# A two-block transformer on one core: transfer scratch of 1 KB instead of 16, and the room given to more places for weights

## The chip, the core and the metric

The kernel runs on one core of one Trainium2 chip. The metric is the device time of one launch in microseconds (us), as a median of several runs. The engines are TensorE (PE, matrix products), VectorE (DVE), ScalarE (ACT), GpSimd (POOL) and SyncE (SP, which does nothing but issue transfers). Each engine works through its own queue of instructions in order; ACT and POOL can issue transfers too.

## The reference, cut to what matters

The input is a sequence of 256 tokens of width 2048. A first block with adaptive modulation, four kinds of attention and 16 experts is followed by a second block with a long convolution ("hyena"), a spatial gate and a feed-forward part. All of it is in fp32.

```python
def first_block(x, c, ...):
    c_act = jax.nn.silu(c)
    mod = c_act @ ada_w[l] + ada_b[l]                 # 2048 x 12288: the modulation
    sh1, sc1, g1, sh2, sc2, g2 = jnp.split(mod, 6, axis=-1)
    h = rmsnorm(x, norm1_g[l]) * (1.0 + sc1[:, None]) + sh1[:, None]
    x = x + g1[:, None] * token_mixer(h, w_in[l], ...)     # dilated, banded, MoBA and NSA attention
    h = rmsnorm(x, norm2_g[l]) * (1.0 + sc2[:, None]) + sh2[:, None]
    x = x + g2[:, None] * moe_ffn(h, router_w, ...)        # 16 experts, 2048 -> 512 -> 2048
    return rmsnorm(x, final_g)

def compress(t, pe, w1, w2):                          # in the NSA attention: blocks of 32 keys, step 16
    blk = (t[:, :, cidx] + pe).reshape(b, hk, n_cmp, NSA_CMP_BLOCK * hd)
    return jax.nn.gelu(blk @ w1) @ w2

def _hyena_mixer(p, conv_w, conv_b, k_f, bias):       # in the second block
    v, x1, x2 = ...
    z = x1 * _long_conv(v, k_f[:, 0], bias[0])        # rfft, times k_f, irfft
    return x2 * _long_conv(z, k_f[:, 1], bias[1])
```

## The kernel before, in words

The work of one launch runs through these stages; the times are those of the profiled execution. `phase0` (0 to about 165 us) computes the first modulation vectors and the filters of the hyena part and projects the first queries, keys and values. `mixers` (to about 630 us) does the four attentions and the output projection, and the rest of the modulation beside them. Then come the router, `overflow` (a branch that runs only where a group of experts has more tokens than fit) and `experts` (about 650 to 1265 us). `block2` does the hyena part (about 1290 to 1525 us), the gate, the merge and the feed-forward part.

A weight comes in pieces of 128 x 1024 fp32 numbers, 512 KB, and each is loaded by one transfer that SP issues in `rload` (L180) into the ring `wraw` with `nraw` = 5 places. Products in fp32 are made of three products of the parts of a number: `split` lets ACT write the upper part `whi` (L146) and DVE the rest `wlo` (L149), each with three places, and `mm3` (L158 to L160) multiplies them. A place of `wraw` is free when DVE has written `wlo`.

The modulation has its own pieces of the same size, 192 of them, in `ada_steps`: the load at L446 into one of four places of the tag `a`, then four matmuls on PE into `ps_ada` (L452), or, in some steps, DVE instead (L456). These steps are called between the steps of other work through a hook, so the loads of pieces and those of weights alternate on SP.

Before the router, `first_chunks` loads 18 weight pieces of the experts in advance: 5 into the ring and 13 into places of other tiles that are idle then. The experts' other loads follow through the ring of five.

`cmp_blocks` (L883 and on) copies keys and values so that blocks of 32 can be read, with two memsets and eight transfers on POOL into the tile `kk`. `long_conv` (L1484 and on) runs four times; it loads one set of filters `kft` by three transfers on ACT's queue (L1487: 1 MB, L1489: 254 KB, L1490: 2 KB) and multiplies it with the transformed input, by way of `cu` and `cv`, one place each.

The order on each engine is set by a scheduler that runs when the program is built: it goes by priorities and by when a place comes free in its own account. More places thus change the order also where the code reads the same. At launch the order is fixed, and only waits on other engines decide when an instruction starts. Each transfer of SP and ACT also has one of eight completion counters (`DMAHW0` to `DMAHW7` in the order with its waits), given out in turn: a transfer that gets a counter waits until the one that had it has landed.

Of the kernel before, what the change touches and what calls it, by code (L numbers as in the profile page):

```python
# [9 lines left out]
F32 = mybir.dt.float32  # L10
# [8 lines left out]
P = 128  # L19
# [120 lines left out]
class Body:  # L140
# [30 lines left out]
    def rload(self, src, kt, n, tag=None):  # L171

        if tag:
            raw = self.piece([P, 1024], tag)
        elif isinstance(self.rawring, tuple):
            pool, tag, bufs = self.rawring
            raw = pool.tile([P, 1024], F32, name="wraw", tag=tag, bufs=bufs)
        else:
            raw = self.rawring
        self.nc.sync.dma_start(raw[:, :n].rearrange("p (k n) -> p k n", k=kt), src)  # L180
        return raw
# [145 lines left out]
    def run(self):  # L327
        ctx, tc, nc, i = self.ctx, self.tc, self.nc, self.i
        self.nraw, self.nsplit = 5, 3
        self.ahead, self.turn = {}, None  # L330
        self.const = ctx.enter_context(tc.tile_pool(name="const", bufs=1, reuse_waits="tile"))
        self.res = ctx.enter_context(tc.tile_pool(name="res", bufs=1, reuse_waits="tile"))
        self.wp = ctx.enter_context(tc.tile_pool(name="wts", bufs=1, reuse_waits="tile"))
        self.rawring = (self.wp, "wraw", self.nraw)
        self.tmp = ctx.enter_context(tc.tile_pool(name="tmp", bufs=2))
        self.dram = ctx.enter_context(tc.tile_pool(name="scratch", bufs=1, reuse_waits="tile", space=DRAM))

        warm = self.tmp.tile([P, 8], F32, name="warm", tag="tms", bufs=2)
        nc.vector.memset(warm, 0.0)
        nc.scalar.activation(warm, warm, AF.Silu)  # L340
        n = 4 * P + sum(WIDTHS.values())
        vec = self.const.tile([P, n], F32, name="vec")
        nc.sync.dma_start(vec, i["p_vec"])
        self.ident, self.lt, self.iota, self.ones = (vec[:, n * P:(n + 1) * P] for n in range(4))
        self.v, n = {}, 4 * P
        for k, m in WIDTHS.items():
            self.v[k] = vec[:, n:n + m]
            n += m
        self.xT = self.res.tile([P, KD, S], F32, name="xT")

        cr = ctx.enter_context(ExitStack())
        self.rt = cr.enter_context(tc.tile_pool(name="route", bufs=1, reuse_waits="tile"))
        self.shift(self.rt)

        self.lp = cr.enter_context(tc.tile_pool(name="pieces", bufs=1, reuse_waits="tile"))
        with ExitStack() as c1:
            self.pp = c1.enter_context(tc.tile_pool(name="ps1", bufs=1, reuse_waits="tile", space=PSUM))
            self.banks = {"mm": 3, "ada": 1, "b": 4}
            self.awp = c1.enter_context(tc.tile_pool(name="awts", bufs=1, reuse_waits="tile"))
            self.phase0()  # L360
            self.mixers()
        with ExitStack() as c2:
            self.pp = c2.enter_context(tc.tile_pool(name="ps2", bufs=1, reuse_waits="tile", space=PSUM))
            self.banks = {"y": 4, "g": 1, "u": 1, "b": 2}
            self.moe()
        cr.close()
        with ExitStack() as c3:
            self.pp = c3.enter_context(tc.tile_pool(name="ps3", bufs=1, reuse_waits="tile", space=PSUM))
            self.banks = {"mm": 4, "b": 4}
            self.block2()  # L370
# [64 lines left out]
    def ada_steps(self, seg, b, dve=False):  # L435


        nc, w = self.nc, self.i["ada_w"][0]
        c0 = seg * D + b * 512
        sb = self.awp.tile([P, 512], F32, name="arow", tag="arow", bufs=1)  # L440
        ps = None if dve else self.bank("ada")
        for q in range(4):
            for h in range(2):
                k0 = 4 * q + 2 * h
                raw = self.piece([P, 2, 512], "a")
                self.last_ada = nc.sync.dma_start(raw, w[k0 * P:(k0 + 2) * P, c0:c0 + 512]  # L446
                                                  .rearrange("(k p) n -> p k n", p=P))
                for j in range(2):
                    k, r = k0 + j, raw[:, j]
                    if not dve:  # L450
                        m = 32 * (2 * h + j)
                        nc.tensor.matmul(ps[m:m + 32], self.cact[:, k], r, start=q == 0, stop=q == 3)  # L452
                    elif k == 0:
                        nc.vector.tensor_scalar(sb, r, self.cs[:, k:k + 1], None, OP.mult)
                    else:
                        nc.vector.scalar_tensor_tensor(sb, r, self.cs[:, k:k + 1], sb, OP.mult, OP.add)  # L456
            if q < 3:
                yield
        n = seg * 16 + b * 4
        bias, mod = self.v["ada_b"][:, n:n + 4], self.mod[:, seg, b * 4:b * 4 + 4]  # L460
        pt = self.bank("ada")
        if dve:
            for a in range(4):
                nc.tensor.matmul(pt[:, a:a + 1], sb[:, a * P:(a + 1) * P], self.ones[:, 0:1], start=True, stop=True)
            nc.vector.tensor_tensor(mod, pt[:, :4], bias, OP.add)
        else:
            nc.vector.tensor_copy(sb, ps)
            pt = pt.rearrange("p (a q) -> p a q", a=4)
            for a in range(4):
                nc.tensor.transpose(pt[:, a], sb[:, a * P:(a + 1) * P], self.ident)  # L470
            s = self.tmp.tile([P, 4], F32, name="adas", tag="modg", bufs=2)
            nc.vector.tensor_reduce(s, pt.rearrange("p a (j r) -> p a r j", r=32)[:, :, 0], AX.X, OP.add)
            nc.vector.tensor_tensor(mod, s, bias, OP.add)
        yield
# [408 lines left out]
    def cmp_blocks(self, n, src):  # L883

        nc, mp = self.nc, self.mp
        kk = mp.tile([P, 2, S], F32, name="kk", tag="s", bufs=3)
        nc.gpsimd.memset(kk[64:, :, 255:], 0.0)
        for h in range(2):
            nc.gpsimd.dma_start(kk[:64, h], src[h * 64:h * 64 + 64])
            nc.gpsimd.dma_start(kk[64:, h, :255], src[h * 64:h * 64 + 64, 1:])  # L890
        blk = mp.tile([P, 16, 2, 16], F32, name="blk", tag="s", bufs=3)
        nc.gpsimd.memset(blk[:, :, :, 15:], 0.0)
        for h in range(2):
            v = kk[:, h].rearrange("p (n j s) -> p s j n", s=2, j=8)[:, 0]
            for a in range(2):
                js = slice(a * 8, a * 8 + 8)
                nc.vector.tensor_tensor(blk[:, js, h, :15], v[:, :, a:a + 15],
                                        self.pe[n][:, js, None].to_broadcast([P, 8, 15]), OP.add)
        return blk
# [297 lines left out]
    def moe(self):  # L1197
        nc, tc, i = self.nc, self.tc, self.i
        with ExitStack() as c0:
            self.mp = c0.enter_context(tc.tile_pool(name="moe", bufs=1, reuse_waits="tile"))  # L1200
            mp = self.mp
            wg, wu, wd = (i["exp_w_" + n][0] for n in ("gate", "up", "down"))
            self.overflow(wg, wu, wd)

            def prepare(p, tag):

# [79 lines left out]
                return work  # L1286
            self.turn = 0
            self.experts([group(g) for g in range(4)], lambda n: (wg[n], wu[n], wd[n]), step, finish)
            self.turn = None
            sums = last["sums"]  # L1290
            self.v1, self.v2 = (self.tmp.tile([P, 8], F32, name="tms", tag="tms", bufs=2) for _ in range(2))
            row = mp.tile([2, S], F32, name="sums")
# [190 lines left out]

    def long_conv(self, o, hf, z, gate):  # L1484
        nc, hp = self.nc, self.hp
        kf = hp.tile([P, 5, 512], F32, name="kft", tag="kft", bufs=1)
        nc.scalar.dma_start(kf[:, :4], self.kf[o, hf])  # L1487

        nc.scalar.dma_start(kf[1:, 4], self.kf[o, hf, 1:, 0])  # L1489
# [11 lines left out]
        for j in range(2):  # L1501
            zr, zi = self.bank("b"), self.bank("b")
            for ps, f in ((zr, j), (zi, 2 + j)):
                for t in range(2):
                    self.mm3(ps, [x[:, t, f * P:(f + 1) * P] for x in self.F], [x[:, t] for x in zt], t == 0, t == 1)
            A, B, Dm = kf[:, j], kf[:, 2 + j], kf[:, 4 if j == 0 else 1]
            for ps, q, c1, c2, op in ((zr, zi, A, B, OP.subtract), (zi, zr, Dm, B, OP.add)):
                u = hp.tile([P, 512], F32, name="cu", tag="cu", bufs=1)
                v = hp.tile([P, 512], F32, name="cv", tag="cv", bufs=1)
                tt(u, ps, c1, OP.mult)  # L1510
                tt(v, q, c2, OP.mult)
                tt(u, u, v, op)
                f = j if op == OP.subtract else 2 + j
                self.split(yf[0][:, f], yf[1][:, f], u)
# [90 lines left out]
```

## Time and profile before

| what | us |
|---|---|
| median of 3 runs (2706.68 to 2711.35) | 2710.29 |
| the profiled execution, its own time | 2719.55 |
| its span in the trace | 2717.8 |
| PE busy in the span | 2608.4 (96%) |
| DVE busy | 1795.3 (66%) |
| ACT busy | 1334.9 (49%) |
| moved by DMA: 640.81 MB, a mean of 236 GB/s | |

A busy PE is not PE at its peak: matmuls are pipelined, and one that is counted as 0.40 us can be followed by the next after 0.23 us. Where a stage waits is therefore read from when the instructions start and from what each engine waited for, not from the busy share. The page gives the span in 40 slices of 68 us, the share of each engine in tenths, and the chain of waits that ended last. A window view gives the same for a stretch, with the mean clock that PE was granted (1.00 is full speed).

### The profile page before, as it was taken

Reading aid. Unit: us, or ns where it says so; the run is one execution under the profiler, and the core shown is the slowest. Engines: PE = TensorE matmul, PEld = TensorE weight load, DVE = VectorE, ACT = ScalarE, POOL = GpSimd, SP = SyncE. Lnnn points to the kernel's source line nnn. Section 1 sums busy time; section 2 is a strip of 40 time slices with the busy share of each in tenths; the row PEclk is TensorE's granted clock in tenths of the full one; section 3 lists DMA queues with packets and bytes.
Section 4 is the critical chain, followed back from the end, with each engine's and each line's share of the span. In section 5 each row is a group of like instructions: output and inputs, shape, how many; then the busy total and the mean of one; then the engine's idle time right before and its main releaser. Section 6 shows DMA issues by size and latency. Waiting matters only on the chain.

```text
span 2717.8 us, 43662 instructions
## 1 busy us (share of the span) xinstructions
PE 2608.4 (96%) x17355; PEld 2261.0 (83%) x17355; DVE 1795.3 (66%) x2509; ACT 1334.9 (49%) x1774; POOL 5.5 (0%) x20
## 2 busy tenths in 40 slices
PE   5998999998999999999999899999999999999997
PEld 1466888887778777776998799999999999998886
DVE  4546877877889888887777655555655555555444
ACT  2333444546777766766443444444444444443443
POOL 0000000000000000000000000000000000000000
PEclk7998999998999999999999899999999999999999
DMA  8888898983899999997554355555555656566664
GB/s 296 286 294 286 281 317 309 331 295 119 297 319 312 324 315 330 331 330 270 184 169 149 127 187 187 187 186 186 186 186 187 189 184 193 186 191 197 193 194 140
DMA packets 320083, 640.81 MB, mean 236 GB/s; under 512 B 21564, under 2 KB 35420, under 8 KB 319104
## 3 DMA queue, kind: packets, MB, share of 16 engines
q1 hardware_dynamic: 310768, 618.83, 68.5%
q10 hardware_dynamic: 8848, 18.61, 2.0%
q8 instruction: 137, 2.24, 0.3%
q0 software_dynamic: 256, 0.52, 0.1%
q14 instruction: 74, 0.61, 0.1%
HBM read 631.01 MB, written 6.35 MB: 235 GB/s over the span
## 4 chain that ended last, share of the span: by engine, by line
PE 56%; DMA 9%; DVE 6%; ACT 3%; issue 1%; ACTq 1%; DVEq 0%; SPq 0%
PE ps_mm L158 16%; PE ps_mm L160 16%; PE ps_mm L159 16%; DVE wlo L149 4%; DMA wraw<-in_exp_w_down_dram 4%; DMA wraw<-in_exp_w_up_dram 4%; ACT whi L146 3%; DMA wraw<-in_exp_w_gate_dram 2%; PE ps_u L159 1%; PE ps_u L160 1%; PE ps_u L158 1%; ACTq L1490 1%; PE ps_g L158 1%; PE ps_g L159 1%; PE ps_g L160 1%
## 5 line engine op out<-in xcount | busy, mean ns | idle before, releaser
L149 DVE TENSOR_TENSOR wlo<-wraw,whi 128x1024 fp32r<-128x1024 f32 (+1 forms) x972 | 1165.7, 1205 | 703.2 <-ACT whi L146 689.4
L146 ACT ACTIVATE whi<-wraw 128x1024 fp32r<-128x1024 f32 (+1 forms) x972 | 1012.3, 1044 | 1021.0 <-PE ps_mm L159 531.9
L158 PE MATMUL ps_mm<-hH,whi 128*128 128x256 f32 x3216 | 910.9, 283 | 9.2 <-ACT whi L146 7.8
L160 PE MATMUL ps_mm<-hH,wlo 128*128 128x256 f32 x3216 | 907.8, 283 | 4.0 <-DVE wlo L149 4.0
L159 PE MATMUL ps_mm<-hL,whi 128*128 128x256 f32 x3216 | 904.2, 281 | 0.0
L158 PEld LDWEIGHTS ps_mm<-hH,whi 128*128 128x128 f32 x3216 | 607.9, 189 | 33.3 <-ACT whi L146 15.2
L160 PEld LDWEIGHTS ps_mm<-hH,wlo 128*128 128x128 f32 x3216 | 605.5, 189 | 19.0 <-DVE wlo L149 9.3
L159 PEld LDWEIGHTS ps_mm<-hL,whi 128*128 128x128 f32 x3216 | 605.7, 188 | 5.2 <-issue 4.8
L159 PE MATMUL ps_mm<-wlo,actH 128*128 128x512 f32 x352 | 137.2, 390 | 0.0
L160 PE MATMUL ps_mm<-whi,actL 128*128 128x512 f32 x352 | 137.0, 389 | 0.0
L158 PE MATMUL ps_mm<-whi,actH 128*128 128x512 f32 x352 | 137.0, 390 | 0.0
L159 PE MATMUL ps_y<-wlo,piece 128*128 128x512 f32 x256 | 105.6, 412 | 8.5 <-DVE wlo L149 7.9
L452 PE MATMUL ps_ada<-piece,cact 128*32 128x512 f32 x512 | 102.2, 650 | 9.4 <-DMA piece<-in_ada_w_dram 8.8
L160 PE MATMUL ps_y<-whi,piece 128*128 128x512 f32 x256 | 101.3, 397 | 0.2 <-DVE piece L149 0.2
L158 PE MATMUL ps_y<-whi,piece 128*128 128x512 f32 x256 | 91.6, 398 | 2.9 <-ACT piece L146 1.9
L456 DVE SCALAR_TENSOR_TENSOR arow<-piece,cs,arow 128x512 f32<-128x512 f32 x120 | 89.4, 745 | 2.1 <-DMA piece<-in_ada_w_dram 1.3
L159 PEld LDWEIGHTS ps_mm<-wlo,actH 128*128 128x128 f32 x352 | 66.1, 188 | 14.0 <-DVE wlo L149 0.3
L158 PEld LDWEIGHTS ps_mm<-whi,actH 128*128 128x128 f32 x352 | 66.1, 188 | 13.7
L160 PEld LDWEIGHTS ps_mm<-whi,actL 128*128 128x128 f32 x352 | 66.1, 188 | 13.5
L159 PEld LDWEIGHTS ps_y<-wlo,piece 128*128 128x128 f32 x256 | 48.3, 189 | 33.4 <-DVE wlo L149 23.3
L158 PE MATMUL ps_mm<-mgH,whi 128*128 128x256 f32 x256 | 71.9, 281 | 0.0
L159 PE MATMUL ps_mm<-mgL,whi 128*128 128x256 f32 x256 | 71.9, 281 | 0.0
(447 smaller groups left out, 3497.9 us busy)
## 6 DMA issues: line engine op xcount, KB each, us to landing
wraw<-in_w_in_dram SPq DMA_DIRECT2D x224, 512.0 KB, 4.6
piece<-in_ada_w_dram SPq DMA_DIRECT2D x192, 512.0 KB, 5.0
wraw<-in_w_ffn_in_dram SPq DMA_DIRECT2D x176, 512.0 KB, 4.5
wraw<-in_exp_w_down_dram SPq DMA_DIRECT2D x125, 512.0 KB, 5.7
wraw<-in_exp_w_up_dram SPq DMA_DIRECT2D x124, 512.0 KB, 5.2
wraw<-in_exp_w_gate_dram SPq DMA_DIRECT2D x122, 512.0 KB, 5.1
wraw<-in_w_ffn_out_dram SPq DMA_DIRECT2D x88, 512.0 KB, 4.2
wraw<-in_w_out_dram SPq DMA_DIRECT2D x64, 512.0 KB, 5.1
```

What stands on the lines that cost most here:

```text
L146: self.nc.scalar.activation(dst, src, AF.Copy)
L149: self.nc.vector.tensor_tensor(dst, src, h.bitcast(F32), OP.subtract)
L158: mm(ps, a[0], b[0], start=start, stop=False)
L159: mm(ps, a[0], b[1], start=False, stop=False)
L160: mm(ps, a[1], b[0], start=False, stop=stop)
L452: nc.tensor.matmul(ps[m:m + 32], self.cact[:, k], r, start=q == 0, stop=q == 3)
L456: nc.vector.scalar_tensor_tensor(sb, r, self.cs[:, k:k + 1], sb, OP.mult, OP.add)
L1490: nc.scalar.dma_start(kf[0:1, 4], self.nyq[o, hf])
```

## The change

The program is built with 1 KB of scratch for transfers that POOL prepares in software, where it was 16 KB in each partition by default. The copies of `cmp_blocks`, the only such transfers, are issued by ACT instead, and their memsets done by DVE. The room that comes free holds: three more places for modulation pieces (tag `a2`, so seven in turn), three more places for the experts' weights (tag `wraw2`, taken in turn with the five from the end of `overflow` on), and second places for `kft`, `cu` and `cv` in the hyena part.

```diff
@@ rload
         elif isinstance(self.rawring, tuple):
             pool, tag, bufs = self.rawring
+            if self.more:
+
+                here, at = self.more
+                self.more = here, (at + 1) % (bufs + 3)
+                if at < 3:
+                    pool, tag, bufs = here, "wraw2", 3
             raw = pool.tile([P, 1024], F32, name="wraw", tag=tag, bufs=bufs)
@@ ada_steps
-                raw = self.piece([P, 2, 512], "a")
+                self.nada += 1
+                raw = (self.piece([P, 2, 512], "a") if self.nada % 7 < 4 else
+                       self.awp.tile([P, 2, 512], F32, name="piece", tag="a2", bufs=3))
@@ cmp_blocks
-        nc.gpsimd.memset(kk[64:, :, 255:], 0.0)
+        nc.vector.memset(kk[64:, :, 255:], 0.0)
         for h in range(2):
-            nc.gpsimd.dma_start(kk[:64, h], src[h * 64:h * 64 + 64])
-            nc.gpsimd.dma_start(kk[64:, h, :255], src[h * 64:h * 64 + 64, 1:])
+            nc.scalar.dma_start(kk[:64, h], src[h * 64:h * 64 + 64])
+            nc.scalar.dma_start(kk[64:, h, :255], src[h * 64:h * 64 + 64, 1:])
         blk = mp.tile([P, 16, 2, 16], F32, name="blk", tag="s", bufs=3)
-        nc.gpsimd.memset(blk[:, :, :, 15:], 0.0)
+        nc.vector.memset(blk[:, :, :, 15:], 0.0)
@@ moe
             self.overflow(wg, wu, wd)
+            self.more = mp, 0
...
-            self.turn = None
+            self.turn = self.more = None
@@ long_conv
-        kf = hp.tile([P, 5, 512], F32, name="kft", tag="kft", bufs=1)
+        kf = hp.tile([P, 5, 512], F32, name="kft", tag="kft", bufs=2)
...
-                u = hp.tile([P, 512], F32, name="cu", tag="cu", bufs=1)
-                v = hp.tile([P, 512], F32, name="cv", tag="cv", bufs=1)
+                u = hp.tile([P, 512], F32, name="cu", tag="cu", bufs=2)
+                v = hp.tile([P, 512], F32, name="cv", tag="cv", bufs=2)
@@ the build
-    nc = bacc.Bacc("TRN2", target_bir_lowering=False, num_devices=1)
+    nc = bacc.Bacc("TRN2", target_bir_lowering=False, num_devices=1, dynamic_dma_scratch_size=1024)
```

The order of the instructions also changes. First, SP's queue behind the weights of the compression (`in_nsa_cmp_w_v`), in the compressed attention; `in_ada_w` are modulation pieces, `in_w_in` the projection's weights. Before:

```order
L908 DMA wraw<-in_nsa_cmp_w_k_dram 128x8x128
L908 DMA wraw<-in_nsa_cmp_w_v_dram 128x8x128 x2
L446 DMA piece<-in_ada_w_dram 128x2x512 x2
L180 DMA wraw<-in_w_in_dram 128x2x512
L446 DMA piece<-in_ada_w_dram 128x2x512 x6
L180 DMA wraw<-in_w_in_dram 128x2x512
L446 DMA piece<-in_ada_w_dram 128x2x512 x2
L180 DMA wraw<-in_w_in_dram 128x2x512
L446 DMA piece<-in_ada_w_dram 128x2x512 x2
L180 DMA wraw<-in_w_in_dram 128x2x512 x2
L446 DMA piece<-in_ada_w_dram 128x2x512 x7
```

And now:

```order
L186 DMA wraw<-in_w_in_dram 128x16x24
L916 DMA wraw<-in_nsa_cmp_w_k_dram 128x8x128 x2
L916 DMA wraw<-in_nsa_cmp_w_v_dram 128x8x128 x2
L454 DMA piece<-in_ada_w_dram 128x2x512 x16
L186 DMA wraw<-in_w_in_dram 128x2x512
L454 DMA piece<-in_ada_w_dram 128x2x512 x2
L186 DMA wraw<-in_w_in_dram 128x2x512 x2
```

Sixteen pieces stand in one row, where five loads of w_in stood between the first sixteen.

Second, ACT's queue in the hyena part with its waits (the names in brackets; `kft` is a filter set, `kf_d` and `nyq_d` its places in memory), from the head of `block2`. Before, the first set stands alone there and the second comes behind the products of the first convolution:

```order
L1487 DMA kft<-kf_d 128x2048 [waits DVE_49]
L146 ACTIVATE yfH<-cu 128x512 [waits DVE_49]
L1489 DMA kft<-kf_d 127x512
L1490 DMA kft<-nyq_d 1x512
L146 ACTIVATE whi<-wraw 128x1024 [waits DMAHW7_49,PE_49,Activation_49]
```

And now, the second set at the head of `block2`:

```order
L1496 DMA kft<-kf_d 128x2048
L146 ACTIVATE whi<-wraw 128x1024 [waits DMAHW1_49,PE_49]
L1498 DMA kft<-kf_d 127x512 [waits DMAHW2_49]
L1499 DMA kft<-nyq_d 1x512 [waits DMAHW3_49]
L146 ACTIVATE whi<-wraw 128x1024 [waits PE_49,Activation_49]
```

The second set moved ahead of the first convolution, with loads of w_in to split behind it, and the third and the fourth stand where the second and the third stood.

Third, SP's queue ahead of the branch of `overflow`, whose first row is the load of `ovi`. Before:

```order
L180 DMA piece<-in_exp_w_down_dram 128x1024
L180 DMA piece<-in_exp_w_up_dram 128x2x512
L180 DMA wraw<-in_exp_w_gate_dram 128x2x512 x5
L1303 TENSOR_LOAD ovi
L1304 COMPARE_AND_BRANCH
```

And now:

```order
L186 DMA piece<-in_exp_w_up_dram 128x2x512
L186 DMA wraw<-in_exp_w_gate_dram 128x2x512 x5
L186 DMA wraw<-in_exp_w_up_dram 128x2x512
L1312 TENSOR_LOAD ovi
L1313 COMPARE_AND_BRANCH
```

One load of `exp_w_up` moved ahead of the branch. Fourth, ACT's queue now has the eight copies of `cmp_blocks`, each with a wait:

```order
L897 DMA kk<-piece 64x256 [waits DMAHW5_49,Activation_49]
L898 DMA kk<-piece 64x255 [waits DMAHW6_49]
L897 DMA kk<-piece 64x256 [waits DMAHW7_49]
L898 DMA kk<-piece 64x255 [waits DMAHW1_49]
L897 DMA kk<-piece 64x256 [waits DMAHW2_49,Activation_49]
L898 DMA kk<-piece 64x255 [waits DMAHW3_49]
L897 DMA kk<-piece 64x256 [waits DMAHW5_49]
L898 DMA kk<-piece 64x255 [waits DMAHW6_49]
```

They stood on POOL; the last two wait for the counters of the first two.

## Rows read from the trace of the kernel before

**Rows 1.** The page: engines' busy time, PE in tenths per slice, GB/s per slice.
```profile
PE 2608.4 (96%) x17355; PEld 2261.0 (83%) x17355; DVE 1795.3 (66%) x2509; ACT 1334.9 (49%) x1774; POOL 5.5 (0%) x20
...
PE   5998999998999999999999899999999999999997
...
GB/s 296 286 294 286 281 317 309 331 295 119 297 319 312 324 315 330 331 330 270 184 169 149 127 187 187 187 186 186 186 186 187 189 184 193 186 191 197 193 194 140
```

**Rows 2.** The page: the chain that ended last, shares of the span.
```profile
PE 56%; DMA 9%; DVE 6%; ACT 3%; issue 1%; ACTq 1%; DVEq 0%; SPq 0%
```

**Rows 3.** Waits of SP's queue, whole span: us in total, times, longest.
```profile
SPq L180 <- DVE wlo L149: 1542.1, 786, 14.9
SPq L446 <- PE ps_ada L452: 184.7, 71, 7.3
```

**Rows 4.** Windows: stretch, busy per engine (instructions), PE's clock, DMA share, GB/s.
```profile
0.00:170.00 170.00, 137.59 (x664) 61.01 (x664) 86.34 (x182) 46.36 (x77) 1.00 (x10) 0.90 0.84 293
...
200.00:250.00 50.00, 43.27 (x357) 33.92 (x355) 28.16 (x54) 15.04 (x27) 0.00 (x0) 0.86 0.90 292
...
605.00:610.00 5.00, 5.00 (x44) 4.82 (x43) 3.35 (x7) 2.32 (x5) 0.00 (x0) 1.00 1.02 383
...
640.00:660.00 20.00, 10.63 (x65) 10.41 (x66) 12.87 (x54) 7.95 (x15) 0.00 (x0) 0.63 0.09 30
...
690.00:1265.00 575.00, 553.66 (x2427) 426.26 (x2426) 486.13 (x471) 408.30 (x422) 0.00 (x0) 1.00 0.93 322
...
1020.00:1040.00 20.00, 19.54 (x84) 14.70 (x83) 17.30 (x16) 14.39 (x14) 0.00 (x0) 1.00 0.99 350
```

**Rows 5.** Groups of DVE's instructions, 690 to 1265 us, the largest.
```profile
L149 DVE TENSOR_TENSOR wlo<-wraw,whi 128x1024 fp32r<-128x1024 f32 x353 | 428.6, 1223 | 84.8 <-ACT whi L146 77.2
```

**Rows 6.** The chain in the experts, 1050 to 1062 us: start, us, what.
```profile
1051.67 5.91 DMA wraw<-in_exp_w_up_dram
...
1057.68 1.07 ACT whi L146
...
1058.78 1.24 DVE wlo L149
```

**Rows 7.** PE in order of time, in the experts and in the tail: start, us.
```profile
800.27 0.40 PE L158 MATMUL ps_g<-whi,xg 128*128 128x512 f32 x1
...
800.98 0.40 PE L158 MATMUL ps_g<-whi,xg 128*128 128x512 f32 x1
...
2000.13 0.28 PE L158 MATMUL ps_mm<-hH,whi 128*128 128x256 f32 x1
2000.25 0.28 PE L159 MATMUL ps_mm<-hL,whi 128*128 128x256 f32 x1
```

**Rows 8.** SP's queue in order of time: start, from first issue to last.
```profile
2.12 42.80 SPq L446 DMA_DIRECT2D piece<-in_ada_w_dram  x20
...
211.94 14.37 SPq L446 DMA_DIRECT2D piece<-in_ada_w_dram  x6
...
654.75 21.94 SPq L180 DMA_DIRECT2D wraw<-in_exp_w_up_dram  x7
```

**Rows 9.** POOL in order of time, one of its eight issues for `kk`.
```profile
183.83 0.52 POOL L890 DMA_DIRECT2D kk<-piece  x1
```

**Rows 10.** ACT's queue and PE in the hyena part, in order of time.
```profile
1294.61 0.33 ACTq L1487 DMA_DIRECT2D kft<-kf_d  x1
...
1300.61 0.32 ACTq L1490 DMA_DIRECT2D kft<-nyq_d  x1
...
1408.32 0.35 ACTq L1487 DMA_DIRECT2D kft<-kf_d  x1
...
1409.31 7.07 ACTq L1490 DMA_DIRECT2D kft<-nyq_d  x1
...
1487.49 6.91 ACTq L1490 DMA_DIRECT2D kft<-nyq_d  x1
...
1496.72 0.49 PE L158 MATMUL ps_b<-ztH,k_dftH 128*128 128x512 f32 x1 [2.49 <-ACT ztH L146]
```

More of the change, by code (lines that the diff above doesn't have):

```diff
@@ L329, in run @@
         self.nraw, self.nsplit = 5, 3
-        self.ahead, self.turn = {}, None
+        self.ahead, self.turn, self.more, self.nada = {}, None, None, 0
         self.const = ctx.enter_context(tc.tile_pool(name="const", bufs=1, reuse_waits="tile"))
```

## The prediction

> **What bounds the kernel now.** I read the page's busy shares first: TensorE (PE) is busy for 2608.4 of 2717.8 us [rows 1]. From about 1565 us on, slice after slice but the last moves 184 to 197 GB/s [rows 1], far less than earlier, and PE stays at 9 tenths until the last [rows 1], so the last 1150 us belong to PE and the change touches nothing there. The chain of waits puts 56% on PE and 9% on DMA [rows 2]; that 9% (245 us) is where places in a ring can matter. The queue's own waits then say what holds the loads back: SP waits 1542.1 us for VectorE (DVE) to finish `wlo`, which frees a ring place, and, with the modulation pieces of L446, 184.7 us for PE at L452 [rows 3]. Last I read the windows [rows 4] stage by stage: the stage decides, not the mean.
>
> The sum is made against the profiled execution, 2719.55 us, and carried over to the median, 2710.29 us, which lies 9.26 us (0.34%) lower. That difference I leave as it is.
>
> **Experts, the largest term.** In 690 to 1265 us DMA moves 322 GB/s [rows 4], and 353 loads were split there [rows 5]: 575 / 353 = 1.63 us a load. The chain shows why [rows 6]: one place is turned round in 5.91 + 1.07 + 1.24 = 8.22 us (transfer, `whi`, `wlo`), and five places give 1.64 us a load. That is what is measured, so the ring is the bound. Eight places at 8.22 us would give 1.03 us a load, so something else becomes late. Three candidates stand close together. DVE: 486.13 us busy / 353 = 1.38 us a load [rows 4, 5]. PE: six 512-column matmuls a load, three steps of them in 0.71 us [rows 7], so 1.42 us, and 2427 - 6 x 353 = 309 smaller ones at 0.12 us [rows 7], 0.10 us a load more: 1.52 us. DMA: the best window within this stage moves 350 GB/s with the engines 99% busy, 524288 B / 350 = 1.50 us; with a longer queue, at 605 to 610 us, 383 GB/s, 1.37 us [rows 4]. The floor is thus 1.52 us, a gain of 575 - 353 x 1.52 = 38 us; were every step of PE the 0.23 us of the shortest in those rows, 1.48 us and 53. The lower bound is that transfers only queue longer: the rate goes to 328, 10 us. With PE, DVE and DMA all near or above 90% not every gap closes: I take three quarters of 38, **29 us**, bounds 10 and 50.
>
> By the Trainium skill ("DMA: Bandwidth & Descriptors", Specifications) a core gets about 358 GB/s from memory; as an estimate that alone would let the stage's bytes through in 575 x 322 / 358 = 517 us, a gain of 58. The trace does not agree with it as a ceiling: 383 GB/s stands in [rows 4].
>
> Before the stage, SP stands at the branch of `overflow` and issues its next load at 654.75 us [rows 8], and 640 to 660 moves 30 GB/s [rows 4]. In the new order one further load stands ahead of the branch and two more places are free behind it. Three loads at 1.5 us are 4.5 us of supply; PE is still waiting for the router then, so I take **3 us** (0 to 5).
>
> **Modulation pieces at the start.** The first 20 pieces take SP 42.80 us [rows 8], 2.14 us each, with four places. At 383 GB/s [rows 4] they would take 1.37 us each, 27.4 in all: 15 us less. Over 0 to 170 us the engines are busy 84% [rows 4]; filling the rest would give 27 us. But PE sits idle there for other reasons too (filters, norms), so the low bound is 5. I take **15 us**, the row of the 20 loads being the nearest. The order of SP's first rows is unchanged, so only the waits go.
>
> **Modulation pieces in the mixers.** The new order moves work here: behind the compression weights SP issues 16 pieces in one row, where w_in loads stood between them. Queued behind them is the next w_in load, and PE waits for that. Five w_in loads stood among the first 16 of the pieces; each gives PE 24 matmuls of 256 columns, 0.12 us apart [rows 7], 2.8 us: 14 us of matmuls that filled the gaps of the compressed attention between 222 and 257 us. The 16 pieces bring 64 matmuls of their own forward, some 7.7 us. If the attention's chain is as long as before, 14 - 7.7 = 6 us of idle time is added. Today PE is busy 43.27 of 50 us there with its clock at 0.86 [rows 4], so cover is thin. On the other side, pieces that are done early no longer stop w_in loads: the six pieces at 211.94 us held SP 14.37 us [rows 8], and up to 10 us may come back. I take **+5 us** (a loss), bounds -10 and +14.
>
> **Compression copies.** POOL loses eight issues of 0.53 us [rows 9]; nobody else needs POOL. ScalarE (ACT) gets them, at 0.35 us each (the issues in [rows 10]) 2.8 us. In the new order each of them carries a wait for an earlier transfer of the queue it shares with SP, and `whi` for the next w_in load stands behind. ACT holds up to three splits in advance, two of which are 5.6 us of PE work; that covers the issue, not a late transfer. **+1 us**, bounds 0 and +8 (a full SP load's 5.91 us [rows 6], and some of the issues). The two memsets are smaller than an issue: nothing.
>
> **Hyena part.** Here one must look at which wait really goes. ACT's queue shows the third transfer of a filter set, 2 KB, held for 7.07 us, though no tile makes it wait; it is let go 8.1 us after the 1 MB transfer ahead of it was issued, while in the first set, where it follows 6 us later, it takes 0.32 [rows 10]. A second place does not remove that hold; it moves it. The order shows the second set ahead of the first convolution, at about 1303 us; sets three and four stand where two and three stood. So of three holds (the outer ones 7.07 and 6.91 us [rows 10]) the last goes, and one comes at 1303 us, under w_in matmuls with up to three splits done. The last one cost PE 2.49 us of waiting at 1496.72 [rows 10], and behind it matmuls at a lower clock, about as much again: 5 us gained, 2 lost at 1303. The second `cu` and `cv` let DVE start the next product a step early, where ACT and PE wait for it: 2 us. Sum **-5 us**, bounds -14 and +3.
>
> **Sum.** -29 - 3 - 15 + 5 + 1 - 5 = **-46 us**: 2673.6 us for the profiled execution, **2664 us** for the median. The tail behind 1565 us moves along unchanged.
>
> **The rivals.**
> (1) All three engines close up: experts -50 with the early loads, start -27, mixers 0, hyena -14, -91 us: 2619. For it speaks that the ring alone explains 1.63 us a load; against it, that DVE, at 486 of 525 us, would be 93% busy.
> (2) A longer queue only lengthens the transfers: experts -10, start -5, mixers +5, hyena 0: -10, about 2700. For it: 99% of the engines' time at 350 GB/s within the stage [rows 4]. Against it: 383 GB/s in the same program.
> (3) Slower: the 16 pieces in a row starve PE in the compressed attention. At 1.37 us each they need 22 us; five w_in loads in the ring are 14 us of PE work. If those run out before the 17th load lands, PE stands for up to the 14 us of matmuls that filled the gaps, and starts again at the lower clock, of which it lost 14% of 50 us there already [rows 4], so 7 more: +21. With rival 2 elsewhere (-15 without its mixers term) that is +6: 2716. It decides the sign once experts, start and hyena together give less than 21 us.
> (4) The places are not used, since the eight completion counters that the order's waits name let no more than eight transfers be under way in all, and ACT's share them. Five or four places against seven or eight lie within that, so I hold it unlikely: within 5 us of 2710.
>
> **How the numbers follow.** The forecast has 0.52, rival 1 0.13, rival 2 0.20, rival 3 0.09, rival 4 0.06. A measurement of this kernel can tell about 0.2% (5.4 us) from no change. Faster: 0.52 + 0.13 + 0.20 = 0.85; the same 0.06; slower 0.09. The forecast's own terms spread it over 2635 to 2690. Reaching up over rival 2, to 2700, takes in most of its 0.20; reaching down to 2620 takes in about half of rival 1. What is left out is rivals 3 and 4 (0.15) and some of 1: the range is 2620 to 2700.
>
> **What would show it.** In the profile after: loads in the experts about 1.5 us apart at 345 GB/s or more, the stage near 545 us, and SP's waits for `wlo` smaller or unchanged while ACT's waits for `wraw` fall. The first 20 pieces through in about 28 us. The hold on ACT's queue gone at the last set and new near the head of the hyena part. In the compressed attention PE waits for a w_in load behind the row of 16 pieces. Wrong would be: transfers that take 8 us and more in the experts at an unchanged rate (rival 2); or a first w_in load behind the 16 pieces that lands 15 us after PE has run dry (rival 3).

## The result, and the profile after

The changed kernel takes 2666.51 us (median of four runs, 2656.63 to 2671.03) where the kernel before takes 2709.57 us: a ratio of 0.9832, with a 95% interval of 0.9808 to 0.9857. The forecast was 2664 us in a range of 2620 to 2700. A second measurement beside other kernels (e12 below) gave 0.9807 (0.9785 to 0.9828). The median of the kernel before was between 2707.19 and 2718.64 us, up to 0.4% apart, on the chips that were used, so kernels are compared below by their ratio to the runs of the kernel before on the same chip.

The page of the changed kernel answers to [rows 1, 2]: busy times, GB/s per slice, and the chain that ended last.

```profile
PE 2574.6 (97%) x17355; PEld 2259.9 (85%) x17355; DVE 1789.8 (67%) x2513; ACT 1333.9 (50%) x1774; POOL 0.8 (0%) x8
...
GB/s 347 283 307 304 274 319 331 300 316 110 306 334 321 338 340 362 349 369 220 175 168 122 174 182 185 188 186 187 182 190 188 187 188 189 189 188 196 196 191 141
...
PE 71%; DVE 3%; ACT 1%; ACTq 1%; issue 1%; DMA 0%; DVEq 0%
```

DMA had 9% of the chain and now has 0%; PE had 56% and now has 71%. In the experts (slices 11 to 18) the rate rose from 297 to 331 GB/s to 306 to 369. The same in windows, which answers to the 690 to 1265 us of [rows 4], and who waited for whom in that stretch (us in total, times, longest):

```profile
690.00:1225.00 535.00, 531.92 (x2414) 430.09 (x2414) 480.85 (x469) 405.15 (x421) 0.00 (x0) 1.00 0.95 342
```

```profile
ACT whi L146 <- PE ps_u L160: 36.6, 106, 0.9
ACT whi L146 <- PE ps_y L160: 35.1, 95, 2.3
DVE wlo L149 <- ACT whi L146: 32.0, 113, 1.9
ACT whi L146 <- PE ps_g L160: 31.1, 82, 1.3
```

ACT, which splits the weights, now waits for PE to free a place; waits for a load are no longer among the large ones. PE is busy 531.92 of 535 us: that is a stage bound by PE.

Where the 43 us went is read from four places that occur once in every trace: the first product of the compression (`blk`), the router's `logits`, the `sums` behind the last expert, and the gate's first product (`wst`). Each line gives the first and the last start. The changed kernel:

```profile
L920 PE MATMUL ps_b<-wraw,blk x64: 272/273/297, 208.5 to 211.8; 128*32 128x128 f32 x64
...
L733 DVE SCALAR_TENSOR_TENSOR logits<-ps_b,tms,shrw x2: 225/230/234, 625.8 to 626.0; 128x16 f32<-128x16 f32 x2
...
L1302 DVE COPY sums<-ps_g x1: 405/405/405, 1243.7 to 1243.7; 2x256 f32<-2x256 f32 x1
...
L1582 PE MATMUL ps_b<-wst,sv x32: 270/275/508, 1505.4 to 1549.7; 128*128 128x128 f32 x32
```

The kernel before, in the profiled execution that the prediction used:

```profile
L912 PE MATMUL ps_b<-wraw,blk x64: 272/421/423, 223.2 to 228.5; 128*32 128x128 f32 x64
...
L725 DVE SCALAR_TENSOR_TENSOR logits<-ps_b,tms,shrw x2: 223/228/232, 638.9 to 639.0; 128x16 f32<-128x16 f32 x2
...
L1293 DVE COPY sums<-ps_g x1: 404/404/404, 1296.4 to 1296.4; 2x256 f32<-2x256 f32 x1
...
L1573 PE MATMUL ps_b<-wst,sv x32: 270/275/582, 1559.6 to 1603.8; 128*128 128x128 f32 x32
```

By these two traces the gain would be 2717.8 - 2663.7 = 54 us, 11 more than the medians show. A second trace of the kernel before (e8) tells why: it reached `blk` at 212.0 us and not at 223.2. The start of the same kernel, with four places, differed by 11 us between these two executions; nothing here tells why. Later stages differ less: the experts took 651.3 and 648.4 us from `ovi` (the integer at the branch) to `sums`, the hyena part 263.2 and 257.0, the end 1158.2 and 1157.2 us. With two traces of each kernel (before and e8; after and e12) the stages are:

| stage | forecast, us | before (two traces) | changed (two traces) | difference of the means |
|---|---|---|---|---|
| to `logits` (start, copies, mixers) | -15 + 1 + 5 = -9 | 638.9, 630.5 | 625.8, 626.9 | -8.4 |
| `logits` to `sums` (branch, experts) | -3 - 29 = -32 | 657.5, 654.9 | 617.9, 617.3 | -38.6 |
| `sums` to `wst` (hyena) | -5 | 263.2, 257.0 | 261.7, 261.5 | +1.5 |
| `wst` to the end of the span | 0 | 1158.2, 1157.2 | 1158.3, 1158.4 | +0.7 |
| sum | -46 | | | -44.8 |

The sum is right because two errors cancel, which is luck: the experts gave 6.6 us more and the hyena part 6.5 us less than forecast. The first row hides two more. To `blk` the means fall by 9.7 us, where start and copies had -14; from `blk` to `logits` they rise by 1.3 us, where the mixers had +5. Two traces that lie 11 us apart can't settle these two.

### The profile page after: what moved, and what is told of

Its sections match the earlier page's. It is cut to its first block, busy times and chain, and to the rows that moved or that the text cites. A ratio compares the mean times of both kernels' runs of the same rounds, so it can differ in the third digit from the quotient of the medians.

```text
span 2663.7 us, 43632 instructions
## 1 busy us (share of the span) xinstructions
PE 2574.6 (97%) x17355; PEld 2259.9 (85%) x17355; DVE 1789.8 (67%) x2513; ACT 1333.9 (50%) x1774; POOL 0.8 (0%) x8
## 4 chain that ended last, share of the span: by engine, by line
PE 71%; DVE 3%; ACT 1%; ACTq 1%; issue 1%; DMA 0%; DVEq 0%
PE ps_mm L158 16%; PE ps_mm L160 16%; PE ps_mm L159 16%; PE ps_y L159 2%; PE ps_y L160 2%; PE ps_y L158 2%; PE ps_u L159 2%; PE ps_g L159 2%; PE ps_u L160 2%; PE ps_g L158 2%; PE ps_u L158 2%; PE ps_g L160 2%; DVE wlo L149 1%; ACTq L1499 1%; PE ps_b L158 1%
## 5 line engine op out<-in xcount | busy, mean ns | idle before, releaser
L460 PE MATMUL ps_ada<-piece,cact 128*32 128x512 f32 x512 | 93.5, 639 | 4.2 <-DMA piece<-in_ada_w_dram 3.3
L160 PE MATMUL ps_mm<-mgH,wlo 128*128 128x256 f32 x256 | 71.9, 281 | 0.0
```

The source lines that it names most:

```text
L160: mm(ps, a[1], b[0], start=False, stop=stop)
```

## The experiments

Every diff is against the changed kernel, except for e7 (against the kernel before) and the two that repeat a kernel.

**e1: five places in the experts again.**

```diff
-            self.more = mp, 0
+            self.more = None
```

> The changed kernel with the experts' loads back in five places; all else as changed. Theory (the ring of five was the bound): the experts' stage, from the router's integer to the sums behind the last expert, goes back from 611 us to about 651 us, and the whole from 2666.5 to 2700 to 2708 us. Rival (the shorter stage comes from work or room elsewhere, or from the load that was issued ahead of the branch): it stays under 625 us, and the whole under 2680 us.

Measured: 2705.45 us, ratio 0.9990 (0.9969 to 1.0011); `ovi` to `sums` took 651.4 us, against 611.4 in the changed kernel. The theory held. The waits in 690 to 1225 us are those of a ring that is too short: ACT waits for loads.

```profile
DVE wlo L149 <- ACT whi L146: 71.0, 138, 2.2
ACT whi L146 <- DMA wraw<-in_exp_w_down_dram: 37.3, 64, 2.2
ACT whi L146 <- DMA wraw<-in_exp_w_up_dram: 30.6, 58, 2.4
```

**e5: one more place instead of three.**

```diff
-                self.more = here, (at + 1) % (bufs + 3)
-                if at < 3:
-                    pool, tag, bufs = here, "wraw2", 3
+                self.more = here, (at + 1) % (bufs + 1)
+                if at < 1:
+                    pool, tag, bufs = here, "wraw2", 1
```

> The changed kernel with one more place in the experts instead of three (six in turn). Theory A (the ring is the bound only until TensorE is, one turn of a place takes 8.22 us): 8.22 / 6 = 1.37 us a load is already under TensorE's 1.52, so at least three quarters of the 40 us stay: stage at most 621 us, whole 2665 to 2677 us. Theory B (transfers grow longer or bunch up, and each place gives its share): a third of 40 us, stage about 638 us, whole about 2690 to 2695 us.

Measured: 2671.27 us, ratio 0.9855 (0.9814 to 0.9895); the stage took 615.4 us. Theory A held: one place brings 36 of the 40 us, as the turn of a place, 8.22 us [rows 6], over six, 1.37 us, lies under what PE needs. Rival 2 of the prediction falls with it. The window of e5 beside that of e1:

```profile
690.00:1225.00 535.00, 530.45 (x2395) 426.03 (x2394) 477.30 (x463) 401.89 (x415) 0.00 (x0) 1.00 0.96 343
```

```profile
690.00:1225.00 535.00, 518.15 (x2272) 398.31 (x2271) 454.40 (x442) 380.12 (x394) 0.00 (x0) 1.00 0.94 322
```

Six places move 343 GB/s and five 322, and eight no more than six (342, above). Beyond six, PE sets the rate; the other two places bring the last 4 us.

**e2: four places for modulation pieces.**

```diff
-                raw = (self.piece([P, 2, 512], "a") if self.nada % 7 < 4 else
+                raw = (self.piece([P, 2, 512], "a") if True else
```

> The changed kernel with four places for modulation pieces, as before; all else as changed. Theory (the start gains 14 to 15 us by the places, the mixers lose little by the new order): the compression's first product comes at about 223 us instead of 208, and the whole is 10 to 15 us longer, 2676 to 2682 us. Rival (the two cancel: what the start gains the mixers lose by the 16 pieces in one row): within 4 us of 2666.5.

Measured: 2681.83 us, ratio 0.9893 (0.9848 to 0.9938); `blk` at 227.0 us, `logits` at 643.4. The theory held in its numbers: beside the other parts of the change, going back to four places costs 15 us by the medians and 17 at `logits`. Not all of that is the pieces' own: with four places the copies on ACT cost time that they don't cost with seven (under e7).

**e6: seven places for the first 64 pieces, four from then on.** SP's order in the mixers is then that of before, without the row of 16 pieces.

```diff
-                raw = (self.piece([P, 2, 512], "a") if self.nada % 7 < 4 else
+                raw = (self.piece([P, 2, 512], "a") if self.nada % 7 < 4 or self.nada > 64 else
```

> The changed kernel with seven places for the first 64 modulation pieces and four from then on, which gives back the old order of SP's queue in the mixers (no row of 16 pieces). Theory of the forecast (the row of 16 costs 5 us, 14 of missing matmuls less 7.7 brought forward and some given back): the whole is about 5 us shorter, 2658 to 2664 us. Rival (pieces done early pay for it later): the same or up to 6 us longer, 2666 to 2673 us, with the compression's first product still at 208 us and the router later.

Measured: 2665.44 us, ratio 0.9833 (0.9789 to 0.9877); `blk` at 207.8 us, `logits` at 629.3. The whole is the same, as the rival has it: the row of 16 costs nothing that can be measured in the end. It is seen all the same. In 195 to 260 us the changed kernel does 444 matmuls and e6 481 (PE's busy time and count are the first pair after the length):

```profile
195.00:260.00 65.00, 57.91 (x444) 42.49 (x443) 44.43 (x85) 19.89 (x50) 0.00 (x0) 0.92 0.86 295
```

```profile
195.00:260.00 65.00, 60.89 (x481) 46.69 (x480) 46.11 (x86) 22.23 (x51) 0.00 (x0) 0.95 0.87 287
```

So 3 us of PE's time are lost in the compressed attention. From `blk` to `logits`, though, the changed kernel takes 417.3 and 419.6 us (its two traces) and e6 421.5, and the other traces with the row of 16 take 417.1 to 421.9. That pieces which are done early are no longer in the way later would explain it; no run shows it by itself.

**e7: the copies on ACT alone, in the kernel before** (the edits of `cmp_blocks` in the change's diff, nothing else; scratch of 16 KB).

> The kernel before with the copies of the compression issued by ScalarE and the memsets done by VectorE, and nothing else. Forecast: +1 us (0 to +8): within 5 us of the kernel before, 2703 to 2714 us, ScalarE spends 8 x 0.4 to 0.6 us on the issues and one split comes later by that. Rival (the waits on the shared completion counters hold ScalarE until loads of SyncE have landed): a hold of 5 us or more among the issues, and the whole 5 to 10 us longer.

Measured: 2714.47 us, ratio 1.0012 (0.9993 to 1.0031): a loss of 3 us that is not clear of zero. A hold like the rival's is there, of 4.2 us; that it ends when a load of SP lands, no view shows. ACT's queue stands between the third copy's issue, over at 183.88 us, and the fourth's at 188.08 us, and what PE waits for in 165 to 205 us is the split behind it:

```profile
183.27 0.61 ACTq L889 DMA_DIRECT2D kk<-piece  x1
188.08 0.47 ACTq L890 DMA_DIRECT2D kk<-piece  x1
...
190.54 0.61 ACTq L890 DMA_DIRECT2D kk<-piece  x1
```

```profile
PE ps_mm L158 <- ACT whi L146: 8.4, 2, 6.1
```

Of the two waits, one of 2.3 us stands ahead of the copies, and in both traces of before too. The one of 6.1 us behind them is new. e2, with four places and the copies on ACT, has it as well:

```profile
186.93 0.61 ACTq L897 DMA_DIRECT2D kk<-piece  x1
191.02 0.47 ACTq L898 DMA_DIRECT2D kk<-piece  x1
```

```profile
PE ps_mm L158 <- ACT whi L146: 8.1, 2, 5.8
```

In the changed kernel the copies follow each other with one gap of 0.64 us, from 177.98 to 178.62:

```profile
177.37 0.61 ACTq L898 DMA_DIRECT2D kk<-piece  x1
178.62 0.47 ACTq L897 DMA_DIRECT2D kk<-piece  x1
```

ACT starts three splits ahead of them there, at 170.55, 172.02 and 174.17 us, and PE waits for none behind them:

```profile
174.00:184.00 10.00, 10.00 (x85) 9.03 (x84) 5.01 (x12) 3.70 (x6) 0.00 (x0) 1.00 0.84 262
```

So with four places the copies on ACT cost PE 6 us at this place; in the changed kernel they cost nothing that the trace shows. As an estimate from that wait up to 6 of e2's 17 us are theirs (the whole of e7 shows 3), and what the seven places bring against the kernel before is nearer to the 8 to 10 us of the stages above, as far as two traces tell.

**e8: the kernel before once more.**

> The kernel before, unchanged, for a second trace of it: the runs say that five places in the experts cost all of the 43 us and four modulation pieces 15 more, which is more than the whole, and the trace of before was of an execution 10 us above its median. If that execution had lost its 10 us by chance, this trace shows them in one stage: the compression's first product at 210 to 216 us instead of 223, or the mixers shorter by as much. If not (the stages agree within 2 us with the first trace, as the experts' stage does in all traces so far), the sum of 54 us holds and the difference lies between executions with and without a profile.

Measured: 2714.95 us, ratio 1.0024 (1.0001 to 1.0047), which also says how far two measurements of one kernel can lie apart. `blk` came at 212.0 us: the first trace of before had lost 11 us there, by something that differs between executions of one kernel. The first trace's whole span was 18 us longer: 8 at `logits`, 3 more from the experts, 6 from the hyena part and 1 from the end.

**e3: the small transfers of a filter set first.**

```diff
-        nc.scalar.dma_start(kf[:, :4], self.kf[o, hf])
-
-        nc.scalar.dma_start(kf[1:, 4], self.kf[o, hf, 1:, 0])
         nc.scalar.dma_start(kf[0:1, 4], self.nyq[o, hf])
+        nc.scalar.dma_start(kf[1:, 4], self.kf[o, hf, 1:, 0])
+        nc.scalar.dma_start(kf[:, :4], self.kf[o, hf])
```

> The changed kernel with the three transfers of a filter set in the other order: the 2 KB one first, then the 254 KB one, the 1 MB one last. Theory (the third transfer is held because the 1 MB one ahead of it is still being taken in): no issue on ScalarE's queue lasts over 1 us except perhaps the last of a set, the hold of 14.5 us behind the first splits shrinks to less than 6, and the hyena stage (sums to the gate's first product) goes from 262 to 250 to 256 us; the whole 2655 to 2662 us. Rival (the hold is for a transfer of another set or engine to land): the holds stay 5 to 14 us, and the whole within 3 us of 2666.5.

Measured: 2659.81 us, ratio 0.9807 (0.9784 to 0.9831), and a hyena stage of 260.3 us. The time lies in the range that the theory gave, but the theory fell: the hold stays 14 us, and now it is the 1 MB transfer that is held. ACT's queue in order of time:

```profile
1253.85 0.22 ACTq L1496 DMA_DIRECT2D kft<-nyq_d  x1
1254.11 0.27 ACTq L1497 DMA_DIRECT2D kft<-kf_d  x1
1254.41 14.16 ACTq L1498 DMA_DIRECT2D kft<-kf_d  x1
```

What is held is whatever comes behind the 127-row transfer of the second set (for how long, the last section says).

**e4: one place for the filter set.**

```diff
-        kf = hp.tile([P, 5, 512], F32, name="kft", tag="kft", bufs=2)
+        kf = hp.tile([P, 5, 512], F32, name="kft", tag="kft", bufs=1)
```

> The changed kernel with one place for the filter set again; the second places of cu and cv stay. Forecast (a second place moves the holds: one of three gone, one new at the head, 3 us in all): the hyena stage is 2 to 4 us longer than the 262 us of the changed kernel, the whole 2668 to 2671 us. Rival (the new hold of 14.5 us at the head costs as much as the one that went, or more): the hyena stage is the same or up to 5 us shorter, 2661 to 2667 us.

Measured: 2664.04 us, ratio 0.9824 (0.9801 to 0.9848); a stage of 264.0 us. The stage fits the forecast and the whole fits the rival; 2.4 us in one trace is less than the 6 us by which two traces of before differ in this stage. Undecided by the times; the second place is worth nothing that can be measured here. The windows are clearer: with one place no hold stands at the head, and PE is busy there as in the kernel before, while the convolutions show none of the changed kernel's gain (its windows stand in the section on the prediction):

```profile
1242.00:1332.00 90.00, 89.20 (x756) 89.01 (x756) 64.91 (x111) 40.94 (x48) 0.00 (x0) 1.00 0.66 201
1332.00:1467.00 135.00, 125.19 (x834) 114.78 (x833) 102.01 (x173) 56.71 (x87) 0.00 (x0) 0.97 0.42 134
```

So it is the second place of `kft` that loses at the head and gains behind; the second places of `cu` and `cv`, which stay here, bring nothing that shows.

**e9: the filter sets on SP's queue** (`nc.scalar` replaced by `nc.sync` in the three transfers).

> The changed kernel with the filter sets (two places) loaded by SyncE's queue instead of ScalarE's. Theory (what costs in the hyena part is that ScalarE cannot split weights while an issue on its queue is held): no hold on ScalarE is left, TensorE's wait of 7.6 us behind the hold of 14.5 us goes, and the hyena stage (sums to the gate's first product) falls from 261.7 to 246 to 254 us; the whole 2650 to 2660 us. Rival (a hold on SyncE's queue delays the w_in loads just as much): the stage stays at 258 to 266 us and the whole within 5 us of 2666.5.

Measured: 2665.32 us, ratio 0.9813 (0.9790 to 0.9835); a stage of 261.4 us. The rival held. SP is held now, with w_in loads behind it, and PE waits as long (8.1 us against 7.4):

```profile
1251.38 1.51 SPq L1498 DMA_DIRECT2D kft<-kf_d  x1
1253.35 12.46 SPq L186 DMA_DIRECT2D wraw<-in_w_in_dram  x1
1265.86 1.30 SPq L1499 DMA_DIRECT2D kft<-nyq_d  x1
```

```profile
PE ps_mm L158 <- ACT whi L146: 8.1, 1, 8.1
```

**e10: the copies on POOL with 4 KB of scratch**, and one place for the filter set, so that it fits.

> The changed kernel with the compression's copies issued by GpSimd again, 4 KB of scratch, and one place for the filter set (so that it fits); to be compared with e4_kft1, 2664.0 us, which has the copies on ScalarE. Theory (the copies on ScalarE cost 5 to 9 us, as the trace of the copies alone has TensorE waiting 8.4 us for splits behind them): the compression's first product 4 to 8 us earlier than the 204 to 212 us of the kernels with seven places, the router's logits at 617 to 623 us instead of 626 to 630, the whole 2655 to 2661 us. Rival (with seven places the loads are far enough ahead that the counters do not hold ScalarE): no difference beyond 3 us, the logits at 626 to 630 us.

Measured: 2666.20 us, ratio 0.9808 (0.9783 to 0.9834); `blk` at 205.3 us, `logits` at 622.4, a hyena stage of 267.4. The whole is the rival's; the logits fit the theory but come at the edge of the spread of the kernels with seven places and copies on ACT (622.5 to 630.3 in seven other traces), and in e11, which has the copies on POOL too, they come at 631.3. With seven places the copies on ACT cost nothing measurable, in line with PE's full window under e7.

**e11: both, e10 with the filter sets on SP.**

> The changed kernel with the compression's copies on GpSimd and 4 KB of scratch, and the filter sets (one place) on SyncE's queue. If both theories hold, 5 us at the start and 8 to 12 in the hyena part: 2650 to 2656 us. If only the one on the hyena part holds: 2655 to 2660 us. If neither: 2664 to 2668 us.

Measured: 2659.84 us, ratio 0.9782 (0.9762 to 0.9802), a stage of 261.0 us. It is the lowest ratio of all, but its interval overlaps that of the changed kernel beside it, and neither part showed a gain alone. I don't count it as better.

**e12: the changed kernel once more.**

> The changed kernel, unchanged, beside the three above and for a second trace. Expected: 2662 to 2671 us; experts' stage 611 us and tail 1144 us as in all traces of it so far, hyena stage 257 to 266 us, the compression's first product at 204 to 212 us. If the first product comes at 215 us or later, the start varies as much with seven places as with four, and its gain is not measurable from single traces.

Measured: 2665.91 us, ratio 0.9807 (0.9785 to 0.9828); `blk` at 207.3 us, experts 611.5, hyena 261.5. All as expected, except that the end takes 1158.4 us, as in the first trace (1158.3): the 1144 of the expectation is not counted from `wst`. With seven places ten traces reached `blk` at 204.2 to 211.6 us; with four places it was 212.0 and 223.2, and 227.0 and 228.3 with the copies on ACT.

## Why the prediction was right, point by point

**Experts: the mechanism was right, the term too small.** The floor of 1.52 us a load came from PE's steps [rows 5, 7]. I then took three quarters of the 38 us, since PE, DVE and DMA were all near their limits. That cut by a quarter was the step that failed: the stage gave 38 to 40 us from `ovi` to `sums` (before and e1 against the changed kernel), all of it. In 690 to 1225 us 349 loads were split, 1.53 us a load, where the floor had been 1.52. DVE at 480.85 of 535 us, 90%, keeps up with PE at 99%. The separate 3 us for the branch can't be seen: in the 58 us from `ovi` on, PE is busy 51.26 us in the changed kernel and 51.34 us before. Rival 1 had 50 us here, rival 2 10, and rival 4, that more places are not used, falls with the same measurement.

**The rate of memory.** The Trainium skill ("DMA: Bandwidth & Descriptors", Specifications) would, as an estimate from its 358 GB/s, have let the stage through in 517 us. The stage moves 342 GB/s, but PE, not DMA, sets that: e5 has 343 with fewer places. So no run here says what the limit of the memory is in this stage.

**Start: right in sign, too large in size.** The first 20 pieces now take SP 35.10 us, where [rows 8] had 42.80: 8 us, not 15. The step that failed is the rate: 1.37 us a piece was that of 383 GB/s in a short stretch elsewhere, and the pieces came at 1.76.

```profile
2.12 35.10 SPq L454 DMA_DIRECT2D piece<-in_ada_w_dram  x20
...
195.86 28.18 SPq L454 DMA_DIRECT2D piece<-in_ada_w_dram  x16
224.09 0.46 SPq L186 DMA_DIRECT2D wraw<-in_w_in_dram  x1
```

What the start as a whole gained is about 8 to 10 us by the means of two traces; the 17 us of e2 contain the hold of the copies (e7). I also took too lightly that a stage with waits on loads everywhere has no fixed length. The row of the 20 loads is not to blame for that: in e8 the same loads took 44.29 us, and `blk` still came 11 us earlier than in the trace that I worked from.

**Mixers: the loss is seen at its place and not in the whole.** The row of 16 took SP 28.18 us, not 22, and no w_in load was issued before 224.09 us. PE lost 3 us by it (e6), where I had forecast 5; in the whole e6 and the changed kernel have the same ratio, so the term is 0 within what can be measured, not +5. Rival 3 put its price on the same place; that it left out that the pieces have to be done some time anyway is the likely reason, and not shown.

**Copies: the cover that I named holds in the changed kernel and not in the kernel before.** I counted on splits in advance to cover the issues, but not a late transfer. In the changed kernel the eight issues take from 175.53 to 181.03 us, three splits were started ahead of them, and PE waits for nothing. In e7 the queue stood 4.2 us between two copies, and PE waited 6.1 us behind them. The bounds of 0 to +8 took in both.

**Hyena part: the step that failed is the price of the hold that I moved to its head.** I said 5 us gained behind, 2 lost in front, 2 more by `cu` and `cv`. The gain is there: in the convolutions PE is busy 132.82 of 135 us and had been 127.88 (129.88 in e8). The 2 us of `cu` and `cv` are not (e4). The loss is 8 us: in the 90 us ahead of them PE is busy 81.30 and had been 89.19. Changed kernel, then before:

```profile
1243.00:1333.00 90.00, 81.30 (x671) 80.43 (x670) 58.01 (x106) 35.67 (x42) 0.00 (x0) 0.96 0.57 187
1333.00:1468.00 135.00, 132.82 (x923) 122.76 (x922) 109.54 (x180) 62.75 (x94) 0.00 (x0) 1.00 0.45 145
```

```profile
1296.00:1386.00 90.00, 89.19 (x757) 89.12 (x757) 64.80 (x111) 41.02 (x48) 0.00 (x0) 1.00 0.62 201
1386.00:1521.00 135.00, 127.88 (x836) 116.67 (x835) 103.18 (x166) 54.52 (x82) 0.00 (x0) 0.96 0.43 139
```

ACT's queue in the changed kernel shows a hold of 14.52 us, where I had expected 7 under three splits of cover:

```profile
1247.39 0.48 ACTq L1498 DMA_DIRECT2D kft<-kf_d  x1
...
1250.22 2.68 ACTq L1496 DMA_DIRECT2D kft<-kf_d  x1
...
1253.05 1.17 ACTq L1498 DMA_DIRECT2D kft<-kf_d  x1
1254.26 14.52 ACTq L1499 DMA_DIRECT2D kft<-nyq_d  x1
```

PE's longest wait of the stage stands behind it:

```profile
PE ps_mm L158 <- ACT whi L146: 7.4, 1, 7.4
```

I took the length of the old holds for a property of the third transfer. It is that of what is queued ahead of it (the last section), and with the second set issued 8 us behind the first, the 127 rows of the first set were queued ahead as well.

## What to carry to other kernels

A ring's rate is one turn of a place over the number of places; add places until that lies under the slowest engine's time for a load, and expect little from more: here one of three brought 36 of 40 us. When a wait is moved by an earlier issue, work out what is queued ahead of it at the new place, since its length moves with the queue. And take a stage that waits for loads all along from two traces before building a sum on it: one kernel's start differed by 11 us between two executions, its hyena part by 6, its experts by 3 and its end by 1.

## What the runs showed of the hardware

What makes the hold at the head of the hyena part so long is one slow transfer ahead of it. From 1262 us on DMA moves 25 to 27 GB/s and its share is 0.06 to 0.07, about one sixteenth, and still does when ACT has been let go at 1254.26 + 14.52 = 1268.78 us; the windows of the changed kernel:

```profile
1263.00:1264.00 1.00, 0.00 (x0) 0.00 (x0) 0.00 (x0) 0.00 (x0) 0.00 (x0) 1.00 0.06 25
...
1266.00:1267.00 1.00, 0.00 (x0) 0.00 (x0) 0.00 (x0) 0.00 (x0) 0.00 (x0) 1.00 0.07 27
...
1269.00:1270.00 1.00, 0.01 (x1) 0.01 (x1) 0.03 (x1) 1.00 (x2) 0.00 (x0) 0.50 0.07 27
```

By the share, as an estimate, one of the 16 DMA engines works and 15 stand. The transfer of 127 rows (L1498 in the changed kernel) has 127 x 2048 = 260096 B, which is 10.4 us at 25 GB/s. The trace also holds the single packets of ACT's queue, and they give the order. The rows of the first set, issued at 1247.39 us, go one after the other from 1249.48 to 1264.09 us. Of the 128 packets of the second set's 1 MB all but 8 are through at 1257.44, and these 8 go behind those rows, until 1266.66. Then the rows of the second set go, until about 1279. ACT was let go 2.1 us after the first of them. So the hold behind the second 127-row transfer does not last until that transfer is done, but until just after it has begun, and here a whole 127-row transfer stood ahead of it.

The same reading fits e3: the rows of its second set begin at 1266.49 us, and the held 1 MB transfer goes at 1254.41 + 14.16 = 1268.57. The old holds are shorter, since there only the set's own 1 MB is ahead: in the kernel before, for the hold from 1409.31 to 1416.38 us, the rows begin at 1414.29, when the 1 MB is nearly through (1415.27), and go on until 1424.70. Over the nine holds of 3 us and more in these three traces ACT is let go 1.9 to 4.6 us after the rows begin. What in the queue lets an issue through at that point no run shows.

By the Trainium skill ("DMA: Bandwidth & Descriptors", Why a DMA increments its semaphore by 16 and not by 1) a transfer goes to the largest number of engines, 16 at most, that divides the count of its slowest dimension on both sides, and 127 partitions go to one; the share of 0.06 agrees. With 128 rows loaded and the first one overwritten afterwards the transfer should by that rule spread over all 16 engines, and the long hold should go; whether the holds of 5 to 7 us would go too is open. None of this was tried.
